# Element work of a gated MLP, taken two chunks at a time in stages, with engines kept in source order and the up projections ahead of the down projections

## The chip, the cores and the metric

The kernel runs on one core of a Trainium2 chip. Its time is the device time of one execution in microseconds. The engines are TensorE (PE, with its weight loads as PEld), VectorE (DVE), ScalarE (ACT), GpSimd (POOL) and SyncE (SP), whose queue issues nearly all DMAs. Each engine works through its own queue in the order in which the program was built.

## The reference: what is computed

An encoder of two layers on 256 tokens of width 1024. Each layer has a token mixer (pooling, windowed attention, gates, an output projection) and a gated MLP, each behind an RMSNorm and with a residual sum; a last RMSNorm follows. The change lies in the MLP, D_FF being 2816:

```python
def _conv_ffn(xn, w_up, conv_w, conv_b, w_down):
    a, gval = jnp.split(xn @ w_up, 2, axis=-1)
    a = lax.conv_general_dilated(a, conv_w[:, None, :], ...) + conv_b   # depthwise, width 3, over tokens
    return (jax.nn.gelu(a) * gval) @ w_down
```

All inputs and weights are float32, and the output is float32.

## The kernel before

**Split operands.** Every matmul operand is written as a high part and a low part (float32r each), and three products stand for one float32 product: high by high, high by low, low by high. A weight comes from HBM in loads of 1 MB (tile `raw`, three buffers, issued on SP), each cut into two pieces. A piece is split by one ACT cast (`wh`, L180) and one DVE subtraction (`wl`, L181), both 128x1024. `Weights.get(look)` returns the next piece and splits pieces up to `look` ahead, three as a rule and four in the up projections; five pieces can be alive at once, and `free` releases one. Some pieces have slots of their own in tiles that stand empty at that time.

**The MLP.** The up projections come in blocks of 512 columns: a0 to a4 and g0 to g4 (the convolved branch and the gate), and r5 with the last 256 columns of both. `by_rows` runs a block: four pieces, and for each piece 12 matmuls of 512 columns (two token halves, six products each). After each piece it calls `unit()`. `turn_up` then has DVE transpose the block's two PSUM tiles in 32x32 squares (`up_rows`, L1133), and when a gate block is done, `cross` moves the squares between partitions with 16 DMAs on SP, four with each unit (`up_turned`, L616). From then on channels are on partitions.

**Element work.** The 2816 channels are 22 chunks of 128. `up(f)` does one chunk: ACT copies the branch (L1152) and scales it with the middle tap (L1154), DVE adds the two outer taps (L1155, L1158); ACT squares (L1165), DVE (L1166), ACT takes tanh (L1169), DVE (L1170); DVE multiplies with the gate (L1174); ACT writes the high part (L1177) and DVE the low part (L1178) of the chunk, into a ring of 12 chunks. `CHUNKS` says after which unit each chunk is written into the program, whole, as one run of eleven instructions.

**Down projections.** `residual_mm` takes a chunk and a piece of `w_down` at a time, 12 matmuls of 512 columns again (L524 to L526), into four accumulators. The last four chunks are held, and finish the accumulators in segments (512 and 512 columns for the first half of the tokens, 512, 256 and 256 for the second); behind each segment the residual sum (DVE, L429), its squares (ACT, L431), and, at the end of a half, the norm (POOL L443, DVE L456) and TensorE's transposes of it (L465) follow. In layer 0, `begin_values` puts the first value products of layer 1 between the transposes; their four pieces have slots of their own.

**What sets the order.** The source is traced, and a scheduler then places the instructions on each engine by its own estimate of when each could run, so that the built order of ACT, DVE and PE is not that of the source. `ORDER` sets the order of blocks in the source: four down units (d0) stand between g2 and a3.

Of the kernel before, what the change touches and what calls it, by code (L numbers as in the profile page):

```python
# [10 lines left out]
F32 = mybir.dt.float32  # L11
F32R = mybir.dt.float32r
# [4 lines left out]
P = 128  # L17
# [64 lines left out]
class Weights:  # L82
# [114 lines left out]
    def get(self, look=LOOK):  # L197
# [10 lines left out]
def encoder(ctx, tc, x, w_in, w_pool, pool_scale, w_a, w_b, w_o, norm1, norm2, w_up, conv_w,  # L208
# [29 lines left out]
    for l in range(DEPTH):  # L238
        for g in range(NG):
            c0 = C_V + g * 512  # L240
            slots = (("m2", 0, 2), ("m2", 1, 2), ("ybig",), ("at2",)) if g == 0 else ()
            for j in range(2):
# [25 lines left out]
        for half in HALVES:  # L268
            half_of(w_a[l], 0, half, 2)
            half_of(w_in[l], C_GA, half, 2)  # L270
            half_of(w_b[l], 0, half, 1)
        for c in range(4):
            W.use(rows(w_o[l], c * 256))
        slots = (("v1",), ("ybig",), ("at2",))
        for kind, n in ORDER.split():
            n = int(n)
            for j in range(2):
# [304 lines left out]
    def run(gen):  # L582
        for _ in gen:
            pass

    def v_tile():
        return acc.tile([P, 512], F32, tag="acc", name="v_ps")

# [19 lines left out]
                visit()  # L608
        return ps

    def cross(out, in_):

        for i in range(4):
            for j in range(4):
                a, b = slice(32 * i, 32 * i + 32), slice(32 * j, 32 * j + 32)
                nc.sync.dma_start(out=out[b, i], in_=in_[a, j])  # L616
            yield
# [174 lines left out]
    for l in range(DEPTH):  # L792
# [318 lines left out]

        acth, actl = (
            [
                big.tile([P, n, 2, P], F32R, tag=f"{tag}{j}", name=f"act{tag}{j}")
                for j, n in enumerate((HPG, NH - HPG))
            ]
            for tag in "qk"
        )
        acts = {}

# [3 lines left out]
        def turn_up(kind, n, ps):  # L1124

            if kind != "g":
                pair[:] = (
                    big.tile([P, 4, 2, 2, 4, 32], F32, tag=tags[n % 2], name=name)
                    for tags, name in ((("at2", "ybig"), "up_rows"), (("xn", "v1"), "up_turned"))
                )  # L1130
            rows, out = (a[:, :, int(kind == "g")] for a in pair)
            for t in range(2):
                nc.vector.transpose(  # L1133
                    out=rows[:, :, t].rearrange("p j c r -> p c j r"),
                    in_=ps[t].rearrange("p (c j r) -> p c j r", c=4, j=4),
                )
            turned[kind, n] = out.rearrange("p i t c r -> p c t i r")
            if kind == "g":
                crossing.append(cross(pair[1], pair[0]))
            if kind == "r":  # L1140
                crossing.append(cross(out, rows))

        def blocks_in_order(a):

            return a.rearrange("p (i r t) -> p t i r", i=4, t=2)

        def up(f):
            w0, w1, w2, b = (prm[:, l, j * NF + f : j * NF + f + 1] for j in range(4))
            n, c = divmod(f, 4)
            av, gv = (turned["r", n][:, j + c] if n == 5 else turned[k, n][:, c] for k, j in (("a", 0), ("g", 2)))  # L1150
            a = sm.tile([P, S], F32, tag="u", name="a")
            nc.scalar.copy(out=blocks_in_order(a), in_=av)  # L1152
            y = sm.tile([P, S], F32, tag="s", name="y")
            nc.scalar.activation(y, a, AF.Identity, bias=b, scale=w1)  # L1154
            nc.vector.scalar_tensor_tensor(  # L1155
                out=y[:, 1:], in0=a[:, : S - 1], scalar=w0, in1=y[:, 1:], op0=ALU.mult, op1=ALU.add
            )
            nc.vector.scalar_tensor_tensor(  # L1158
                out=y[:, : S - 1], in0=a[:, 1:], scalar=w2, in1=y[:, : S - 1],
                op0=ALU.mult, op1=ALU.add,  # L1160
            )

            c = float(np.sqrt(2.0 / np.pi))
            y2 = sm.tile([P, S], F32, tag="us", name="y2")
            nc.scalar.activation(y2, y, AF.Square, scale=float(np.sqrt(0.044715)))  # L1165
            nc.vector.scalar_tensor_tensor(  # L1166
                out=y2, in0=y2, scalar=1.0, in1=y, op0=ALU.add, op1=ALU.mult
            )
            nc.scalar.activation(y2, y2, AF.Tanh, scale=c)  # L1169
            nc.vector.scalar_tensor_tensor(  # L1170
                out=y2, in0=y2, scalar=1.0, in1=y, op0=ALU.add, op1=ALU.mult
            )
            g = sm.tile([P, 2, P], F32, tag="p", bufs=3, name="g")
            nc.vector.tensor_mul(out=g.rearrange("p t (i r) -> p t i r", i=4), in0=blocks_in_order(y2), in1=gv)  # L1174
            n = f % NH
            ah, al = (x[n >= HPG][:, n - HPG * (n >= HPG)] for x in (acth, actl))
# [4 lines left out]
            acts[f] = (ah, al)  # L1181

        late = {}
        begun = []

        def begin_values():

            ps, held = v_tile(), [W.get() for _ in range(4)]
# [9 lines left out]
        count, chunk = 0, 0  # L1198

        def unit():  # L1200
            nonlocal count, chunk
            count += 1
            if crossing and next(crossing[0], "end") == "end":
                crossing.pop(0)
            while chunk < NF and CHUNKS[chunk] < count:
                up(chunk)
                chunk += 1

        for kind, n in ORDER.split():
            if kind == "d":  # L1210
                for _ in range(4):
                    next(down)
                    unit()
                continue
            if (kind, n) == ("a", "0"):
# [8 lines left out]
                ps = by_rows(x2, 4, unit, W.LOOK + 1)  # L1224
            n = int(n)
            turn_up(kind, n, ps)
        assert chunk == NF and not crossing
# [36 lines left out]
```

## Time and profile before

| | |
|---|---|
| median of 3 runs | 870.39 us (869.97 to 870.42) |
| profiled execution | 869.86 us, its span 868.1 us |
| granted TensorE clock | 0.999 |
| PE, PEld | 857.6 us, 723.4 us busy |
| DVE, ACT, POOL | 653.1, 484.6, 22.0 us busy |
| HBM read | 160.12 MB, 186 GB/s over the span |

The span reaches from the first to the last instruction of the profiled execution; what is around it is in the execution's time alone. Matmuls are pipelined, so a PE that is busy all the time may still lose time between matmuls: this is read from their starts. Rows of a timeline give the start in us from the span's start, the length in us, engine, source line, operation, tiles written and read, shapes and the count of merged instructions, then in brackets the idle time before and what ended it. Rows of groups give busy time, mean ns of one, then idle time before them and what ended it. An "SPq" row is the issue of a DMA.

### The profile page before, as it was taken

How to read it: one execution, taken by the hardware profiler on the slowest of the kernel's cores; microseconds unless marked ns; L12 is line 12 of the kernel's file. 1: busy time of each engine (PE TensorE's matmuls, PEld its weight loads, DVE VectorE, ACT ScalarE, POOL GpSimd, SP SyncE). 2: the span in 40 equal slices, each digit the busy share in tenths (PEclk: the TensorE clock that was granted, in tenths of full speed). 3: DMA queues.
4: the chain of work that ended last, by engine and by line, in shares of the span. 5: the costliest groups of instructions: out<-in, count | busy, mean ns of one | idle time of the engine just before them, and what ended most of it. 6: DMA issues, size and time to landing. Idle time of an engine off the chain costs nothing.

```text
span 868.1 us, 11702 instructions
## 1 busy us (share of the span) xinstructions
PE 857.6 (99%) x4234; PEld 723.4 (83%) x4234; DVE 653.1 (75%) x1016; ACT 484.6 (56%) x777; POOL 22.0 (3%) x53
## 2 busy tenths in 40 slices
PE   9999999999999999999999999999999999999997
PEld 7888988888888888888788889888888888888876
DVE  6998796756756797969965968775567758968796
ACT  7755554543634666566745555545445436756584
POOL 2020000000000000000000000000000000000000
PEclk9999999999999999999999999999999999999999
DMA  9676646665747777576746556556567377757761
GB/s 334 214 220 220 212 126 215 190 221 169 267 147 224 234 228 236 176 235 209 267 156 207 182 194 194 148 192 211 203 216 260 106 241 239 217 174 237 247 220 48
DMA packets 106942, 178.74 MB, mean 206 GB/s; under 512 B 7982, under 2 KB 49150, under 8 KB 106884
## 3 DMA queue, kind: packets, MB, share of 16 engines
q1 hardware_dynamic: 106372, 176.66, 61.9%
q0 software_dynamic: 496, 1.33, 0.6%
q8 instruction: 33, 0.54, 0.2%
q14 instruction: 25, 0.20, 0.1%
q10 hardware_dynamic: 16, 0.00, 0.0%
HBM read 160.12 MB, written 1.07 MB: 186 GB/s over the span
## 4 chain that ended last, share of the span: by engine, by line
PE 87%; DVE 7%; DMA 2%; SPq 1%; issue 1%; ACT 1%; POOL 0%; POOLq 0%; DVEq 0%; ACTq 0%
PE rows_ps L594 41%; PE proj_ps L497 14%; PE proj_ps L499 7%; PE v_ps L594 6%; DVE wl L181 4%; PE res_ps L525 3%; PE res_ps L526 3%; PE res_ps L524 3%; PE v_ps L784 3%; PE v_ps L697 1%; SPq L616 1%; DMA up_turned<-up_rows 1%; PE o_ps L975 1%; PE s_ps L918 1%; DVE y L1170 1%
## 5 line engine op out<-in xcount | busy, mean ns | idle before, releaser
L181 DVE TENSOR_TENSOR wl<-raw,wh 128x1024 fp32r<-128x1024 f32 x274 | 331.5, 1220 | 128.2 <-ACT wh L180 123.7
L180 ACT CAST wh<-raw 128x1024 fp32r<-128x1024 f32 x274 | 284.2, 1048 | 186.9 <-PE rows_ps L594 94.7
L594 PE MATMUL rows_ps<-wh,x 128*128 128x512 f32 x896 | 279.8, 391 | 0.0
L594 PEld LDWEIGHTS rows_ps<-wh,x 128*128 128x128 f32 x896 | 168.2, 188 | 34.3
L594 PE MATMUL rows_ps<-wl,x 128*128 128x512 f32 x448 | 174.8, 390 | 0.2
L497 PE MATMUL proj_ps<-x,wh 128*128 128x512 f32 x512 | 128.7, 393 | 0.0
L497 PEld LDWEIGHTS proj_ps<-x,wh 128*128 128x128 f32 x512 | 92.1, 189 | 16.4
L594 PEld LDWEIGHTS rows_ps<-wl,x 128*128 128x128 f32 x448 | 84.2, 188 | 18.4 <-DVE wl L181 1.1
L499 PEld LDWEIGHTS proj_ps<-x,wl 128*128 128x128 f32 x512 | 69.9, 190 | 5.1
L499 PE MATMUL proj_ps<-x,wl 128*128 128x256 f32 x512 | 71.6, 283 | 0.0
L525 PE MATMUL res_ps<-wl,actq 128*128 128x512 f32 (+1 forms) x184 | 70.4, 385 | 0.1
L526 PE MATMUL res_ps<-wh,actk 128*128 128x512 f32 (+1 forms) x184 | 70.2, 381 | 0.0
L524 PE MATMUL res_ps<-wh,actq 128*128 128x512 f32 (+1 forms) x184 | 64.8, 382 | 1.0 <-ACT wh L180 1.0
L1133 DVE STREAM_TRANSPOSE up_rows<-rows_ps 128x512 f32<-128x512 f32 x40 | 27.6, 705 | 25.3 <-PE rows_ps L594 21.6
L525 PEld LDWEIGHTS res_ps<-wl,actq 128*128 128x128 f32 x184 | 34.6, 188 | 8.8 <-DVE wl L181 2.2
L524 PEld LDWEIGHTS res_ps<-wh,actq 128*128 128x128 f32 x184 | 34.5, 188 | 8.4 <-ACT wh L180 1.8
L594 PE MATMUL rows_ps<-wh,po 128*128 128x512 f32 x128 | 40.1, 389 | 0.0
L526 PEld LDWEIGHTS res_ps<-wh,actk 128*128 128x128 f32 x184 | 34.6, 188 | 6.3
L1154 ACT ACTIVATE y<-a,prm 128x256 f32<-128x256 f32 x44 | 25.1, 593 | 14.1 <-DVE y L1170 14.1
L1165 ACT ACTIVATE y<-y 128x256 f32<-128x256 f32 x44 | 18.3, 416 | 26.0 <-DVE y L1158 25.8
L594 PEld LDWEIGHTS rows_ps<-wh,po 128*128 128x128 f32 x128 | 24.0, 188 | 5.0
L1177 ACT ACTIVATE actq<-g 128x256 fp32r<-128x256 f32 x44 | 17.6, 415 | 18.7 <-DVE g L1174 18.5
(203 smaller groups left out, 1107.2 us busy)
## 6 DMA issues: line engine op xcount, KB each, us to landing
raw<-in_w_in_dram SPq DMA_DIRECT2D x58, 1024.0 KB, 6.2
raw<-in_w_up_dram SPq DMA_DIRECT2D x40, 1024.0 KB, 5.9
raw<-in_w_down_dram SPq DMA_DIRECT2D x22, 1024.0 KB, 6.7
up_turned<-up_rows SPq DMA_DIRECT2D x160, 64.0 KB, 3.9
raw<-in_w_a_dram SPq DMA_DIRECT2D x8, 1024.0 KB, 4.9
raw<-in_w_o_dram SPq DMA_DIRECT2D x8, 1024.0 KB
pt<-rows SPq DMA_DIRECT2D x64, 64.0 KB, 4.8
raw<-in_w_b_dram SPq DMA_DIRECT2D x4, 1024.0 KB
```

Source lines behind the costliest of these rows:

```text
L180: lambda: nc.scalar.copy(out=h, in_=src),
L181: lambda: nc.vector.tensor_sub(out=l, in0=src, in1=h.bitcast(F32)),
L497: nc.tensor.matmul(ps, wh(k), x2[:, k], start=(k == 0), stop=False)
L499: nc.tensor.matmul(ps[:, 1], wl(k), x2[:, k, 0], start=False, stop=(k == nk - 1))
L524: nc.tensor.matmul(ps, ah, wh, start=first, stop=False)
L525: nc.tensor.matmul(ps, ah, wl, start=False, stop=False)
L526: nc.tensor.matmul(ps, al, wh, start=False, stop=last)
L594: nc.tensor.matmul(ps, x2[:, 2 * n + j, part, t, :], w[:, j, :], start=(n + m == 0), stop=(n == of - 1 and m == 5),)
L784: nc.tensor.matmul(ps[t], a[:, k, t, :], w[:, j, :], start=(k + m == 0), stop=(k == KD - 1 and m == 2),)
L1133: nc.vector.transpose(out=rows[:, :, t].rearrange("p j c r -> p c j r"), in_=ps[t].rearrange("p (c j r) -> p c j r", c=4, j=4),)
L1154: nc.scalar.activation(y, a, AF.Identity, bias=b, scale=w1)
L1165: nc.scalar.activation(y2, y, AF.Square, scale=float(np.sqrt(0.044715)))
```

## The change

- `ORDER` puts all up blocks ahead of the down units, and a new entry v0 behind g0.
- `v0` (layer 0 only) takes two of the four pieces of layer 1's first value columns there, into the tile `m2`, where `begin_values` finds them; the other two stay at the end.
- The element work becomes `two_up(f)`: two chunks in four stages, one stage with each unit. Copies, taps and the multiplication with the gate stay one instruction per chunk; the square, tanh, the two operations behind them, and both halves of the split become one instruction for both chunks, 512 wide. `TWOS` lists the units at which a pair begins.
- The ring holds 16 chunks, the last four in the tiles `v0` and `gates`.
- `keep_order` ties each instruction on PE, ACT and DVE to the one before it in the source, from the first block to the last unit of d4, for order alone, without a semaphore. SP and POOL are left to the scheduler, and so is what follows d4.
- In block a0, `ahead` splits one more piece with each unit. The crossing of r5 begins one unit later.

```diff
-ORDER = "a0 g0 a1 g1 a2 g2 d0 a3 g3 a4 g4 r5 d1 d2 d3 d4"
-CHUNKS = (*range(13, 36, 2), 41, 43, 45, 47, 50, 51, 53, 54, 56, 57)
+ORDER = "a0 g0 v0 a1 g1 a2 g2 a3 g3 a4 g4 r5 d0 d1 d2 d3 d4"
+RING = 16
+TWOS = (16, 20, 24, 28, 32, 36, 39, 43, 47, 51, 55)
...
+    def ahead(self, n):
+        self._split(self.n_got + n)
...
+    def keep_order(engines=("PE", "Activation", "DVE")):
+
+        traced = nc.cur_bb.bb.instructions
+        first = traced[-1]
+        yield
+        start = next(k for k in reversed(range(len(traced))) if traced[k] is first) + 1
+        before = {}
+        for i in traced[start:]:
+            e = i.engine.name
+            if e in engines:
+                if e in before:
+                    info = mybir.DependencyInfo(mybir.DependencyClass.NoSync, mybir.DependencyReason.DATA)
+                    tc.add_manual_dep(i, before[e].name, info, reason="source order")
+                before[e] = i
...
+        def two_up(f):
+
+            a = sm.tile([P, 2, S], F32, tag="u", name="a")
+            yg = sm.tile([P, 4, S], F32, tag="s", name="yg")
+            for j in range(2):
+                w0, w1, w2, b = (prm[:, l, i * NF + f + j : i * NF + f + j + 1] for i in range(4))
+                av, _ = rows_of(f + j)
+                aj, y = a[:, j], yg[:, j]
+                nc.scalar.copy(out=blocks_in_order(aj), in_=av)
+                nc.scalar.activation(y, aj, AF.Identity, bias=b, scale=w1)
+                nc.vector.scalar_tensor_tensor(
+                    out=y[:, 1:], in0=aj[:, : S - 1], scalar=w0, in1=y[:, 1:], op0=ALU.mult, op1=ALU.add
+                )
+                nc.vector.scalar_tensor_tensor(
+                    out=y[:, : S - 1], in0=aj[:, 1:], scalar=w2, in1=y[:, : S - 1],
+                    op0=ALU.mult, op1=ALU.add,
+                )
+            yield
 
             c = float(np.sqrt(2.0 / np.pi))
+            y, g = yg[:, 0:2], yg[:, 2:4]
+            y2 = sm.tile([P, 2, S], F32, tag="us", name="y2")
             nc.scalar.activation(y2, y, AF.Square, scale=float(np.sqrt(0.044715)))
             nc.vector.scalar_tensor_tensor(
                 out=y2, in0=y2, scalar=1.0, in1=y, op0=ALU.add, op1=ALU.mult
             )
+            yield
+
             nc.scalar.activation(y2, y2, AF.Tanh, scale=c)
             nc.vector.scalar_tensor_tensor(
                 out=y2, in0=y2, scalar=1.0, in1=y, op0=ALU.add, op1=ALU.mult
             )
+            for j in range(2):
+                _, gv = rows_of(f + j)
+                gj = g[:, j].rearrange("p (t i r) -> p t i r", t=2, i=4)
+                nc.vector.tensor_mul(out=gj, in0=blocks_in_order(y2[:, j]), in1=gv)
+            yield
...
+            nc.scalar.mul(out=ah, in_=g, mul=0.5)
             nc.vector.scalar_tensor_tensor(
                 out=al, in0=g, scalar=0.5, in1=ah.bitcast(F32), op0=ALU.mult, op1=ALU.subtract
             )
...
+            yield
...
         def unit():
-            nonlocal count, chunk
+            nonlocal count
             count += 1
             if crossing and next(crossing[0], "end") == "end":
                 crossing.pop(0)
-            while chunk < NF and CHUNKS[chunk] < count:
-                up(chunk)
-                chunk += 1
+            if count in TWOS:
+                open_two.append(two_up(2 * len(twos)))
+                twos.append(count)
+            for two in open_two:
+                next(two, None)
...
+            if kind == "v":
+                if l + 1 < DEPTH:
+                    late["pieces"] = [W.get() for _ in range(2)]
+                continue
...
                 for k in range(4):
+                    W.ahead(k + 1)
                     v_sum(ps[1], x2, 1, k, held[k])
                     unit()
```

More of the change, by code (lines that the diff above doesn't have):

```diff
@@ L241, in encoder @@
             slots = (("m2", 0, 2), ("m2", 1, 2), ("ybig",), ("at2",)) if g == 0 else ()
-            for j in range(2):
+            for j in range(l > 0 and g == 0, 2):
                 tag = "k1" if l == 0 and g == 1 and j == 0 else None
@@ L276, in encoder @@
             n = int(n)
+            if kind == "v":
+                if l + 1 < DEPTH:
+                    W.use(rows(w_in[l + 1], 0, 4, C_V, 512), (("m2", 0, 2), ("m2", 1, 2)))
+                continue
             for j in range(2):
@@ L609, in by_rows, with cross @@
         return ps
-    def cross(out, in_):
+    def cross(out, in_, after=0):
+        for _ in range(after):
+            yield
         for i in range(4):
@@ L1113, in encoder @@
             [
-                big.tile([P, n, 2, P], F32R, tag=f"{tag}{j}", name=f"act{tag}{j}")
-                for j, n in enumerate((HPG, NH - HPG))
+                big.tile([P, n, 2, P], F32R, tag=tag, name=f"act{tag}")
+                for tag, n in zip(tags, (HPG, NH - HPG, HPG))
             ]
-            for tag in "qk"
+            for tags in (("q0", "q1", "v0"), ("k0", "k1", "gates"))
         )
@@ L1140, in turn_up, with rows_of @@
             if kind == "r":
-                crossing.append(cross(out, rows))
+                crossing.append(cross(out, rows, 1))
         def blocks_in_order(a):
             return a.rearrange("p (i r t) -> p t i r", i=4, t=2)
-        def up(f):
-            w0, w1, w2, b = (prm[:, l, j * NF + f : j * NF + f + 1] for j in range(4))
+        def rows_of(f):
             n, c = divmod(f, 4)
[L1150 to L1161, printed above, removed]
+            return (turned["r", n][:, j + c] if n == 5 else turned[k, n][:, c] for k, j in (("a", 0), ("g", 2)))
@@ L1163, in up @@
             c = float(np.sqrt(2.0 / np.pi))
-            y2 = sm.tile([P, S], F32, tag="us", name="y2")
+            y, g = yg[:, 0:2], yg[:, 2:4]
+            y2 = sm.tile([P, 2, S], F32, tag="us", name="y2")
             nc.scalar.activation(y2, y, AF.Square, scale=float(np.sqrt(0.044715)))
@@ L1172, in up @@
             )
[L1173 to L1176, printed above, removed]
+            for j in range(2):
[3 more added lines that the diff above has]
+            yield
+            n = f % RING
+            m = (n >= HPG) + (n >= NH)
+            n -= (0, HPG, NH)[m]
+            ah, al = (x[m][:, n : n + 2] for x in (acth, actl))
+            g = g.rearrange("p c (t m) -> p c t m", t=2)
             nc.scalar.mul(out=ah, in_=g, mul=0.5)
@@ L1180, in up @@
             )
-            acts[f] = (ah, al)
+            for j in range(2):
+                acts[f + j] = (ah[:, j], al[:, j])
+            yield
         late = {}
@@ L1186, in begin_values @@
         def begin_values():
-            ps, held = v_tile(), [W.get() for _ in range(4)]
+            ps, held = v_tile(), late["pieces"] + [W.get() for _ in range(2)]
             for n in range(3):
@@ L1197, in encoder @@
         )
-        count, chunk = 0, 0
+        count, twos, open_two = 0, [], []
         def unit():
-            nonlocal count, chunk
+            nonlocal count
             count += 1
@@ L1204, in unit @@
                 crossing.pop(0)
-            while chunk < NF and CHUNKS[chunk] < count:
-                up(chunk)
-                chunk += 1
+            if count in TWOS:
[3 more added lines that the diff above has]
+                next(two, None)
+        ordered = keep_order()
+        next(ordered)
         for kind, n in ORDER.split():
@@ L1214, in encoder @@
                 continue
+            if kind == "v":
+                if l + 1 < DEPTH:
+                    late["pieces"] = [W.get() for _ in range(2)]
+                continue
             if (kind, n) == ("a", "0"):
@@ L1226, in encoder @@
             turn_up(kind, n, ps)
-        assert chunk == NF and not crossing
+        next(ordered, None)
+        assert 2 * len(twos) == NF and not crossing
         if l + 1 < DEPTH:
```

## The prediction

> **What bounds the kernel now.** I read the page first: the engines' shares, then the chain of waits.
>
> ```profile
> span 868.1 us, 11702 instructions
> PE 857.6 (99%) x4234; PEld 723.4 (83%) x4234; DVE 653.1 (75%) x1016; ACT 484.6 (56%) x777; POOL 22.0 (3%) x53
> PE 87%; DVE 7%; DMA 2%; SPq 1%; issue 1%; ACT 1%; POOL 0%; POOLq 0%; DVEq 0%; ACTq 0%
> ```
>
> TensorE carries 87% of the chain. The change leaves every matmul of the kernel in place, so it can win only what TensorE loses between matmuls. The 13% that the chain gives to others are not that loss: while TensorE has weights in stock, a chain through VectorE costs it nothing. So I looked at stages, and then at starts of matmuls.
>
> ```profile
> 263.10:320.00 56.90, 56.90 (x253) 47.15 (x252) 42.14 (x61) 30.34 (x46) 0.00 (x0) 1.00 0.76 241
> 382.00:437.00 55.00, 52.70 (x243) 42.71 (x242) 51.65 (x92) 38.22 (x69) 2.49 (x4) 1.00 0.70 234
> ...
> 263.12 54.40 PE rows_ps L594 x240
> ```
>
> The stage rows give length, then busy time of PE, PEld, DVE, ACT, POOL, the clock, DMA. Early in layer 0's MLP TensorE never stops; late in it VectorE is busy 51.65 of 55.00 us and TensorE falls short. The third line, a piece of the chain, gives the pitch of undisturbed 512-column matmuls: 54.40/240 = 0.2267 us. A weight piece serves 12 of them, 2.72 us; I call that a unit. An MLP has 66 units (44 up, 22 down). Now the loss:
>
> ```profile
> 262.96 0.39 PE L594 MATMUL rows_ps<-wh,x 128*128 128x512 f32 x1
> 432.18 0.28 PE L526 MATMUL res_ps<-wh,actk 128*128 128x256 f32 x1
> 434.20 0.41 PE L465 MATMUL xt_ps<-ident,xn 128*128 128x128 f32 x2 [1.75 <-DVE xn L456]
> 691.00 0.39 PE L594 MATMUL rows_ps<-wh,x 128*128 128x512 f32 x1
> 858.92 0.28 PE L524 MATMUL res_ps<-wh,actq 128*128 128x256 f32 x1
> ```
>
> Unit 5 of layer 0 begins at 262.96. Up to the last 256-column matmul before the norm's transposes stand, by the code, 58 units of 12 and three held segments of 12, 732 matmuls of 512 columns (165.9 us), and eleven of 256. In layer 1 the first 256-column matmul starts at 858.92: 167.92 us, 2.0 over 165.9. In layer 0, 169.22 less 165.9 less eleven at 0.12 (half the columns) leaves 2.0 too. After that TensorE waits for the norm, 434.20 − 432.18 − 0.12 = 1.9 us. So 2.0 + 1.9 + 2.0 = 5.9 us are there to be had, 0.7%, unless something new is broken.
>
> Who causes the 2.0?
>
> ```profile
> 415.91 0.39 PE L526 MATMUL res_ps<-wh,actk 128*128 128x512 f32 x1
> 416.78 1.19 PE L524 MATMUL res_ps<-wh,actq 128*128 128x512 f32 x4 [0.48 <-ACT wh L180]
> 418.38 0.40 PE L526 MATMUL res_ps<-wh,actk 128*128 128x512 f32 x1
> ...
> 344.53 1.03 ACT L180 CAST wh<-raw 128x1024 fp32r<-128x1024 f32 x1
> 348.84 0.72 DVE L1133 STREAM_TRANSPOSE up_rows<-rows_ps 128x512 f32<-128x512 f32 x1 [3.76 <-PE rows_ps L594]
> 349.48 1.18 DVE L181 TENSOR_TENSOR wl<-raw,wh 128x1024 fp32r<-128x1024 f32 x1
> ```
>
> From 415.91 to 418.38 six matmuls take 2.47 us where 1.36 would do: 1.1 us lost for a late split (wh on ACT, wl on DVE). The other kind is in the last rows: ACT's half of a split ends at 345.56, but a transpose put at the head of DVE's queue waits 3.76 us for TensorE, and DVE's half comes at 349.48. Both are matters of order and backlog on ACT and DVE, which the change rewrites.
>
> **The change, part by part.**
>
> *Splits, transposes, element work in source order.* In by_rows a piece is split four units ahead, and its buffer (five of them) is that of the piece just finished. So in source order a transpose waiting for the end of unit u stands ahead of a split that needs the buffer of unit u anyway: nothing that could run is behind it. The 3.76 us wait before a ready split cannot recur in this form. What is left is whether DVE keeps up.
>
> ```profile
> L181 DVE TENSOR_TENSOR wl<-raw,wh 128x1024 fp32r<-128x1024 f32 x274 | 331.5, 1220 | 128.2 <-ACT wh L180 123.7
> L180 ACT CAST wh<-raw 128x1024 fp32r<-128x1024 f32 x274 | 284.2, 1048 | 186.9 <-PE rows_ps L594 94.7
> L1133 DVE STREAM_TRANSPOSE up_rows<-rows_ps 128x512 f32<-128x512 f32 x40 | 27.6, 705 | 25.3 <-PE rows_ps L594 21.6
> L1158 DVE SCALAR_TENSOR_TENSOR y<-a,prm,y 128x255 f32<-128x255 f32 x44 | 20.9, 480 | 0.7
> L1166 DVE SCALAR_TENSOR_TENSOR y<-y,y 128x256 f32<-128x256 f32 x44 | 18.2, 418 | 1.8 <-ACT y L1165 1.7
> L869 DVE SCALAR_TENSOR_TENSOR pd<-us,u 128x512 f32<-128x512 f32 x8 | 5.5, 686 | 0.0
> 383.62 0.75 DVE L1170 SCALAR_TENSOR_TENSOR y<-y,y 128x256 f32<-128x256 f32 x2
> 422.55 3.49 DVE L181 TENSOR_TENSOR wl<-raw,wh 128x1024 fp32r<-128x1024 f32 x3
> ```
>
> Four units (10.88 us) now hold four splits, two transposes and one pair of chunks: four convolution steps, three merged 512-wide operations (priced by L869, the same operation at that width), two multiplies. By whole durations: 4×1.22 + 2×0.705 + 4×0.48 + 3×0.686 + 2×0.418 = 11.1, so DVE would fall behind by 0.2 per four units, about 1.3 us over the six pairs begun at units 16 to 36. But the last two rows show that queued instructions overlap: three splits in 3.49 us are 1.14 each, two 256-wide operations in 0.75 are 0.33 each, 0.085 less than alone. Taking that off all fifteen leaves 9.8, a full us to spare. Stage one beside a block's end can put DVE some 1.5 us late, made good in the next units; a split is due 4×2.72 − 1.05 − 1.22 = 8.6 us after it may begin. Either price hides. In the down phase transposes fall away after unit 44, and pairs come four units apart; DVE has 2 us more. I therefore price the MLP stalls at nothing but a 0.1 us bubble or two.
>
> The Trainium skill (Perfetto Trace Analysis, Optimizing Scalar/DVE Operations) puts DVE's overhead per instruction on SBUF at about 60 ns, the profiled one at about twice that since half overlaps the next; by it each merge saves 60 ns, by the durations above 2×418 − 686 = 150. The overlap in the trace agrees with the page's kind of price. The sum is the same by both, since DVE is hidden by both.
>
> *Value pieces of layer 1 split early (v0).* Two splits (2.4 us DVE, 2.1 ACT) and a 1 MB load move from the end of layer 0's MLP to units 4 to 9, where there is no element work:
>
> ```profile
> 269.69 1.23 DVE L181 TENSOR_TENSOR wl<-raw,wh 128x1024 fp32r<-128x1024 f32 x1 [1.50 <-ACT wh L180]
> 425.62 2.00 ACT L180 CAST m<-raw 128x1024 fp32r<-128x1024 f32 x2 [2.10 <-DMA raw<-in_w_in_dram]
> 428.95 1.05 ACT L180 CAST ybig<-raw 128x1024 fp32r<-128x1024 f32 x1 [1.33 <-DMA raw<-in_w_in_dram]
> 430.86 0.62 ACT L431 ACTIVATE junk<-h 128x512 f32<-128x512 f32 x1
> 428.99 1.28 DVE L429 TENSOR_TENSOR h<-res_ps,h 128x512 f32<-128x512 f32 x2
> 433.57 0.49 DVE L456 SCALAR_TENSOR_TENSOR xn<-h,rstd,gain 128x256 f32<-128x256 f32 x1 [0.44 <-POOL rstd L443]
> ```
>
> DVE has 1.50 us idle per unit there, so two units absorb them; without that cover they would cost 2.4. On SP the load goes ahead of block a1's weights, wanted only at unit 9 (273.9). At the end, the squares (junk) that follow the residual sums of 428.99 are held until 430.86 by casts whose load came late (428.95). The two remaining pieces now take the place of m's, ready by 425.62, and those casts end by 427.6, so the squares start with the sums, about 1.2 us sooner; the rest comes from the split backlog that is gone. The mixer's end runs the same residual code without such casts:
>
> ```profile
> 248.62 0.28 PE L526 MATMUL res_ps<-wh,m 128*128 128x256 f32 x1
> 248.74 0.60 PE L465 MATMUL xt_ps<-ident,xn 128*128 128x128 f32 x4
> ```
>
> There the transposes follow at 0.12, no wait at all. Bounds of this term: 1.2 to 1.9; I take 1.6, nearer the mixer's row.
>
> *Free edits.* The larger ring only lets down projections follow all ups. The down matmuls moved are as many as before. Order on SP and POOL is not imposed.
>
> Sum: 2.0 + 2.0 + 1.6 = 5.6 us. The profiled run took 869.86 (span 868.1 and 1.8 around it); 864.3 by that run. The median is 870.39, 0.5 above it: 864.8.
>
> **Rivals.**
>
> *The norm wait stays* (scheduling behind the loop is not pinned, and ybig's casts may still stand ahead of the squares): gain 4.0 less bubbles, 866.6. For: the same queue mixes both. Against: the load is one place earlier.
>
> *Slower: ACT held by a crossing.* The copy that opens a pair waits for the crossing DMAs of its block, and in forced order the casts queue behind it.
>
> ```profile
> 273.55 1.31 DVE L1133 STREAM_TRANSPOSE up_rows<-rows_ps 128x512 f32<-128x512 f32 x2
> 280.51 6.19 SPq L616 DMA_DIRECT2D up_turned<-up_rows  x8
> 372.36 0.72 DVE L1133 STREAM_TRANSPOSE up_rows<-rows_ps 128x512 f32<-128x512 f32 x1 [0.64 <-PE rows_ps L594]
> 386.63 5.81 SPq L616 DMA_DIRECT2D up_turned<-up_rows  x8
> up_turned<-up_rows SPq DMA_DIRECT2D x160, 64.0 KB, 3.9
> L1154 ACT ACTIVATE y<-a,prm 128x256 f32<-128x256 f32 x44 | 25.1, 593 | 14.1 <-DVE y L1170 14.1
> L1152 ACT COPY a<-up_turned 128x256 f32<-128x256 f32 x44 | 17.0, 416 | 1.6 <-DMA up_turned<-up_rows 1.6
> ```
>
> With 3.9 us to landing, block 0 crossed 280.51 + 6.19 + 3.9 − 274.86 = 15.7 us after its transposes, block 4 took 386.63 + 5.81 + 3.9 − 373.08 = 23.3, SP being held by loads that waited for splits. Blocks 3 and 4 have the least time: transposed behind units 32 and 40, opened at 39 and 47. Unit 47 begins at 262.96 + 42×2.72 = 377.2, its copy may run from 378.3, behind a cast; unit 40 ends at 360.9, the transposes with a lag of 1.5 near 363.7. With 15.7 the copy waits 1.1; with 23.3 until 387.0. Then stage one (2.0: two of 0.593, two of 0.416) and a split (2.3) bring piece 51 at 391.3, wanted at 388.1: 3.2 us lost, and by the same count 0.5 at unit 39. Two layers: 7.4 lost against 5.6 won, 872.2. It turns slower from a crossing of about 22.4 us. Against it: with DVE less behind, the loads that held SP come free sooner. By the Trainium skill's rule that ACT and DVE are strict first-in-first-out queues (Perfetto Trace Analysis, Tensor Engine Instruction), nothing could pass the waiting copy; the 3.76 us row agrees for DVE.
>
> *Nothing happens*: order is not what is missing, the pairs lag as chunks did, 870.
>
> **How the numbers follow.** Forecast 0.70 (864.2 to 866.0), norm wait stays 0.13, nothing 0.05, crossing 0.12. The range runs from 863.5 (all 5.9, and a us of small bubbles around the norms) to 868.0 (norm wait kept and a third of the stalls), which leaves out the last two cases and some tail. About 0.2% (1.7 us) can be told from no change: faster 0.83, same 0.05, slower 0.12.
>
> **What would show it.** Right: between unit 5 and the first 256-column matmul about 166 us in both layers; the transpose wait after layer 0's last held segment under 0.5; DVE's split waiting for ACT, never PE for DVE. Norm rival: 1.75 stays on that row. Crossing rival: ACT's copy waits for up_turned by more than 5 us and PE waits for wh about units 43 and 51. Wrong altogether: PE waits of a kind not listed, or a changed pitch.

## The result, and the profile after

The changed kernel takes 863.91 us in the median (863.62 to 864.34), the kernel before, run beside it, 870.28 us. The ratio is 0.9928, with a 95% interval of 0.991 to 0.9945: faster by 6.4 us. Its profiled execution took 863.69 us, with a span of 861.6. All ratios below are to the kernel before, measured beside each kernel.

First the page of the kernel after: instructions, the engines' busy shares, and the chain of waits by engine.

```profile
span 861.6 us, 11559 instructions
PE 854.1 (99%) x4234; PEld 724.0 (84%) x4234; DVE 651.3 (76%) x950; ACT 487.5 (57%) x711; POOL 20.2 (2%) x53
PE 98%; DMA 0%; ACT 0%; SPq 0%; issue 0%; DVE 0%; POOLq 0%; POOL 0%; DVEq 0%; ACTq 0%
```

TensorE carries 98% of the chain instead of 87%, with the same 4234 matmuls. ACT and DVE have 66 instructions less each, but their busy times have hardly moved (DVE 653.1 to 651.3 us).

The stages of layer 0's MLP in the kernel after (length, then busy time of PE, PEld, DVE, ACT and POOL, the granted clock, DMA share and GB/s):

```profile
263.10:320.00 56.90, 56.90 (x253) 47.12 (x252) 44.20 (x57) 32.56 (x41) 0.00 (x0) 1.00 0.81 267
320.00:382.00 62.00, 62.00 (x276) 51.32 (x275) 59.51 (x90) 45.81 (x66) 0.00 (x0) 1.00 0.73 241
382.00:431.00 49.00, 49.00 (x227) 40.93 (x226) 35.51 (x51) 27.37 (x38) 0.99 (x3) 1.00 0.61 212
```

TensorE is busy throughout. VectorE's crowded stretch is no longer the last one (51.65 of 55.00 us before) but the middle one, 59.51 of 62.00 (46.95 before), and there it costs nothing. Now the starts that the prediction measured by, in the timeline of TensorE after:

```profile
262.95 0.39 PE L617 MATMUL rows_ps<-wh,x 128*128 128x512 f32 x1
428.87 0.28 PE L532 MATMUL res_ps<-wh,actq 128*128 128x256 f32 x1
430.18 0.28 PE L534 MATMUL res_ps<-wh,actk 128*128 128x256 f32 x1
430.30 0.60 PE L473 MATMUL xt_ps<-ident,xn 128*128 128x128 f32 x4
686.47 0.39 PE L617 MATMUL rows_ps<-wh,x 128*128 128x512 f32 x1
852.39 0.28 PE L532 MATMUL res_ps<-wh,actq 128*128 128x256 f32 x1
```

From unit 5 to the first 256-column matmul: 428.87 − 262.95 = 165.92 us and 852.39 − 686.47 = 165.92 us, the time of 732 undisturbed matmuls in both layers. Both losses of 2.0 are gone to the last hundredth. The norm's transposes follow the last segment by 0.12 (430.18 to 430.30), so the wait of 1.9 is gone too. That is 5.9 of the span's 6.5 us; the last 0.6 are small bubbles of 0.1 to 0.2 us, which stood between the transposes and in the value products that follow them.

### The profile page after: what moved, and what is told of

It is laid out like the page before. It is cut to its first block, busy times and chain, and to the rows that moved or that the text cites. A ratio compares the mean times of both kernels' runs of the same rounds, so it can differ in the third digit from the quotient of the medians.

```text
span 861.6 us, 11559 instructions
## 1 busy us (share of the span) xinstructions
PE 854.1 (99%) x4234; PEld 724.0 (84%) x4234; DVE 651.3 (76%) x950; ACT 487.5 (57%) x711; POOL 20.2 (2%) x53
## 4 chain that ended last, share of the span: by engine, by line
PE 98%; DMA 0%; ACT 0%; SPq 0%; issue 0%; DVE 0%; POOLq 0%; POOL 0%; DVEq 0%; ACTq 0%
PE rows_ps L617 43%; PE proj_ps L505 13%; PE proj_ps L507 7%; PE v_ps L617 6%; PE res_ps L532 6%; PE res_ps L534 6%; PE res_ps L533 6%; PE v_ps L809 3%; PE v_ps L722 1%; PE o_ps L1000 1%; PE s_ps L943 1%; PE o_ps L996 1%; PE s_ps L938 1%; PE xt_ps L473 1%; PE pool_ps L499 0%; PE pool_ps L498 0%
## 5 line engine op out<-in xcount | busy, mean ns | idle before, releaser
L617 PEld LDWEIGHTS rows_ps<-wl,x 128*128 128x128 f32 x448 | 84.1, 188 | 17.3
L532 PE MATMUL res_ps<-wh,actq 128*128 128x512 f32 (+1 forms) x152 | 57.5, 378 | 0.0
L533 PE MATMUL res_ps<-wl,actq 128*128 128x512 f32 (+1 forms) x152 | 57.4, 378 | 0.0
L534 PE MATMUL res_ps<-wh,actk 128*128 128x512 f32 (+1 forms) x152 | 57.4, 378 | 0.0
L533 PEld LDWEIGHTS res_ps<-wl,actq 128*128 128x128 f32 x152 | 28.6, 188 | 5.4
L532 PEld LDWEIGHTS res_ps<-wh,actq 128*128 128x128 f32 x152 | 28.6, 188 | 5.4
L534 PEld LDWEIGHTS res_ps<-wh,actk 128*128 128x128 f32 x152 | 28.6, 188 | 5.3
L439 ACT ACTIVATE junk<-h 128x512 f32<-128x512 f32 (+1 forms) x20 | 10.9, 547 | 30.8 <-DVE h L437 30.8
L1185 ACT ACTIVATE yg<-a,prm 128x256 f32<-128x256 f32 x44 | 26.6, 604 | 1.5
L532 PE MATMUL res_ps<-wh,m 128*128 128x512 f32 (+1 forms) x72 | 26.9, 374 | 0.0
```

Of the source, the lines that this page charges most:

```text
L439: nc.scalar.activation(junk[:, 0 : cc.stop - cc.start], h[:, t, cc], AF.Square, scale=D**-0.5, accum_out=ss[:, n : n + 1],)
L532: nc.tensor.matmul(ps, ah, wh, start=first, stop=False)
L533: nc.tensor.matmul(ps, ah, wl, start=False, stop=False)
L534: nc.tensor.matmul(ps, al, wh, start=False, stop=last)
L617: nc.tensor.matmul(ps, x2[:, 2 * n + j, part, t, :], w[:, j, :], start=(n + m == 0), stop=(n == of - 1 and m == 5),)
L1185: nc.scalar.activation(y, aj, AF.Identity, bias=b, scale=w1)
```

## The experiments

Three kinds: parts of the change taken out, parts of it put alone on the kernel before, and the slower rival brought about.

### The forced order taken out of the kernel after

```diff
-        ordered = keep_order()
-        next(ordered)
+        ordered = iter(())
```

> The changed kernel without the ties between instructions: pairs, stages, early value pieces and block order as they are, the order on each engine again the scheduler's. Theory O (order): the stalls inside the MLPs (2.0 us a layer before) come from transposes and element work that stand ahead of splits that could run; without the ties 1 to 2 us a layer return, 866 to 868 us, with PE waiting for wh or wl, and DVE waiting at transposes for several us at a time. Theory L (load): what mattered is that VectorE has less to do and the down units come last; the time stays within 0.5 us of 863.9.

Measured: 871.47 us (869.35 to 874.21), ratio 1.001 (0.9996 to 1.0024). The whole gain is gone. TensorE loses 3.0 us per layer, in one stall; the norm wait stays away. The profiled execution, at 869.35 us, has these stalls at the full clock; what makes others up to 5 us longer is in the last section. The stall's rows in layer 0, from the timelines of ACT, DVE and PE without the order:

```profile
366.72 1.03 ACT L181 CAST wh<-raw 128x1024 fp32r<-128x1024 f32 x1
370.55 0.72 DVE L1158 STREAM_TRANSPOSE up_rows<-rows_ps 128x512 f32<-128x512 f32 x1 [5.52 <-DMA up_turned<-up_rows]
374.24 1.22 DVE L182 TENSOR_TENSOR wl<-raw,wh 128x1024 fp32r<-128x1024 f32 x1
375.51 0.50 PE L533 MATMUL res_ps<-wl,actq 128*128 128x512 f32 x1 [2.74 <-DVE wl L182]
```

ACT's half of the split ends at 367.75, DVE's half starts at 374.24. Between them the scheduler put a transpose that waits 5.52 us for a DMA, and then stage-one work. This is the same kind of stall as the 3.76 us in the kernel before. The stages alone don't cure it.

### The forced order alone, on the kernel before

```diff
+        ordered = keep_order()
+        next(ordered)
...
+        next(ordered, None)
```

> The kernel before with nothing but the ties: element work a whole chunk at a time, CHUNKS, d0 and the value pieces where they were. Theory O: the 2.0 us a layer inside the MLPs go, the norm's wait of 1.9 us stays: 866.4 us (865.8 to 867.2). Theory L: whole chunks in source order make ACT and DVE wait for each other eleven times a chunk, VectorE stays behind, 870 us or slower.

Measured: 948.24 us, ratio 1.0895 (1.0876 to 1.0914): 78 us slower. Theory O was wrong by its whole sign; what came is theory L, far beyond its 870. Three rows of the timeline of DVE, then a wait of ACT for DVE and one of DVE for ACT (total us, times, longest):

```profile
301.22 0.43 DVE L1181 SCALAR_TENSOR_TENSOR y<-y,y 128x256 f32<-128x256 f32 x1 [0.55 <-ACT y L1180]
303.85 1.31 DVE L1148 STREAM_TRANSPOSE up_rows<-rows_ps 128x512 f32<-128x512 f32 x2
318.51 1.31 DVE L1148 STREAM_TRANSPOSE up_rows<-rows_ps 128x512 f32<-128x512 f32 x2
...
ACT y L1180 <- DVE y L1173: 70.6, 44, 2.1
DVE y L1181 <- ACT y L1180: 24.1, 44, 0.8
```

In source order a chunk is a chain of eleven instructions that goes back and forth between ACT and DVE, and nothing else may pass while one waits for the other. A block's four pieces and the two chunks beside them need 318.51 − 303.85 = 14.66 us on DVE, 3.54 of them idle in seven waits for ACT; TensorE needs 4 × 2.72 = 10.88. The loss recurs with every block, and behind the stalls the granted clock falls too (0.977 in the mean of the profiled execution). The scheduler's order of before was not only a nuisance: it filled these gaps.

### All four stages in one unit, order kept

```diff
-                next(two, None)
+                run(two)
```

> The changed kernel, source order kept, but all four stages of a pair in one unit. Each pair then puts some 4.8 us of VectorE work, with ACT and VectorE waiting for each other at four changes of hand (about 0.6 us each), between two splits. A split may be 8.6 us late in the up phase and 5.9 in the down phase, so theory O with its slack expects no more than 1 us over both layers, 863.9 to 864.9 us. A rival: the stages are what keeps VectorE from idling, and without them it falls behind from pair to pair, 867 us or more.

Measured: 897.51 us, ratio 1.0312 (1.0296 to 1.0327). Theory O was wrong again, for the same reason; the rival (867 us or more) came. DVE's timeline with one stage per pair:

```profile
339.93 1.30 DVE L1158 STREAM_TRANSPOSE up_rows<-rows_ps 128x512 f32<-128x512 f32 x2
...
348.34 0.69 DVE L1199 SCALAR_TENSOR_TENSOR y<-y,yg 128x512 f32<-128x512 f32 x1 [0.76 <-ACT y L1198]
349.73 0.69 DVE L1205 SCALAR_TENSOR_TENSOR y<-y,yg 128x512 f32<-128x512 f32 x1 [0.70 <-ACT y L1204]
...
351.92 0.69 DVE L1220 SCALAR_TENSOR_TENSOR actk<-yg,actq 128x512 fp32r<-128x512 f32 x1 [0.70 <-ACT actq L1219]
352.53 1.31 DVE L1158 STREAM_TRANSPOSE up_rows<-rows_ps 128x512 f32<-128x512 f32 x2
```

Three hand-overs from ACT leave DVE idle for 2.16 us per pair. The period is 352.53 − 339.93 = 12.60 us against 10.88. The same place in the kernel after:

```profile
305.04 1.23 DVE L182 TENSOR_TENSOR wl<-raw,wh 128x1024 fp32r<-128x1024 f32 x1 [0.62 <-ACT wh L181]
...
315.92 1.23 DVE L182 TENSOR_TENSOR wl<-raw,wh 128x1024 fp32r<-128x1024 f32 x1 [0.62 <-ACT wh L181]
```

The period is 10.88 us, and DVE's only idle time in it is 0.62: with one stage in each unit, ACT's part runs while DVE does splits. So stages are not a matter of lateness that is made good later; they set whether DVE's work fits into the period at all.

### Stages and order for single chunks, on the kernel before

The kernel before with the order forced and each chunk's eleven instructions in four stages, one per unit. No pairs, no merged instructions, ring of 12, d0 in its old place, value pieces late, and no early splits in block a0.

```diff
+            yield            # behind the taps, the square and the tanh steps of up(f)
...
-                up(chunk)
+                open_up.append(up(chunk))
+            for one_up in open_up:
+                next(one_up, None)
```

> The kernel before with the ties, and with the element work of each single chunk in four stages, one with each unit: no pairs, no merging, ring of 12, d0 and value pieces where they were. Stages with order are then what the gain is made of: nothing lost inside the MLPs, 863.9 to 864.6 us (the single chunk's sequence keeps ACT and VectorE busy at once, as in the pairs that were not merged). Rival: two chunks in a stage are needed to fill the waits between ACT and VectorE; then VectorE falls behind as with whole chunks, 875 us or more.

Measured: 868.93 us (868.71 to 869.57), ratio 0.9986 (0.9977 to 0.9996), between both expectations. By the starts, the MLP loses 2.0 us in each layer, and all of it in one place, which the kernel before doesn't have. DVE's and PE's timelines:

```profile
263.17 0.72 DVE L1148 STREAM_TRANSPOSE up_rows<-v_ps 128x512 f32<-128x512 f32 x1 [0.64 <-PE v_ps L609]
263.81 3.45 DVE L181 TENSOR_TENSOR wl<-raw,wh 128x1024 fp32r<-128x1024 f32 x3
265.05 0.50 PE L609 MATMUL rows_ps<-wl,x 128*128 128x512 f32 x1 [1.69 <-DVE wl L181]
```

The two transposes of block a0 wait for TensorE at the head of DVE's queue, and three splits that could have run long before stand behind them. It is the early splits of block a0 that are missing.

### The early splits of block a0 taken out of the kernel after

```diff
-                    W.ahead(k + 1)
```

> The kernel after without the early splits of block a0 (the splitting of one more piece with each of its four units), everything else as it is. Theory A, source order needs them: with single chunks in stages and the order kept, TensorE waited 1.85 us at 262.97 for the first low half of block g0, because two transposes of a0 that wait for TensorE stood ahead of it on DVE, and the same in layer 1 (2.0 per layer in all). Without the early splits the pairs should show the same wait: 1.8 to 2.0 us per layer at unit 5, 863.9 + 3.7 to 4.0 = 867.5 to 867.9, ratio about 0.997. Rival B, the stall belongs to the single chunks or to the down units left between: no wait at unit 5, 863.4 to 864.4. The prediction priced this edit at nothing and did not say what hides it.

Measured: 867.95 us (867.64 to 868.33), ratio 0.9969 (0.9958 to 0.998). By the starts it loses 2.03 and 1.99 us, at unit 5 of each layer, and nothing elsewhere. ACT's, DVE's and PE's timelines:

```profile
258.82 3.89 ACT L181 CAST wh<-raw 128x1024 fp32r<-128x1024 f32 x4
263.81 0.72 DVE L1158 STREAM_TRANSPOSE up_rows<-v_ps 128x512 f32<-128x512 f32 x1 [0.64 <-PE v_ps L617]
264.45 4.59 DVE L182 TENSOR_TENSOR wl<-raw,wh 128x1024 fp32r<-128x1024 f32 x4
265.69 0.50 PE L617 MATMUL rows_ps<-wl,x 128*128 128x512 f32 x1 [1.69 <-DVE wl L182]
```

ACT's halves of the four splits are done one by one from 259.9 to 262.7. In the kernel after, DVE takes its halves at once, and the transposes of a0 follow at 264.90:

```profile
259.22 4.63 DVE L182 TENSOR_TENSOR wl<-raw,wh 128x1024 fp32r<-128x1024 f32 x4 [0.26 <-ACT wh L181]
```

Theory A holds. One line, about which the prediction says nothing, is worth 4.0 us of the 6.4. It also closes the case of the single chunks: in the MLP they lose 2.03 and 1.98, the same as the pairs without these splits. What is left between the two, about 1 us, lies at the norm at the end of layer 0 and in the value products behind it.

### Value pieces late again, with the order and without it

```diff
-ORDER = "a0 g0 v0 a1 g1 a2 g2 a3 g3 a4 g4 r5 d0 d1 d2 d3 d4"
+ORDER = "a0 g0 a1 g1 a2 g2 a3 g3 a4 g4 r5 d0 d1 d2 d3 d4"
...
-            ps, held = v_tile(), late["pieces"] + [W.get() for _ in range(2)]
+            ps, held = v_tile(), [W.get() for _ in range(4)]
```

> The changed kernel with all four value pieces of layer 1 at the end of layer 0's MLP again. If the early pieces removed the norm's wait (my term of 1.6 us): TensorE waits 1.2 to 1.9 us for xn at the end of layer 0, 865.1 to 865.8 us. If the wait went because the split backlog went: under 0.5 us of wait, 863.9 to 864.4 us.

> The changed kernel without the ties and with all four value pieces at the end of layer 0's MLP. Without the ties but with early pieces the norm's wait was gone and 3.0 us a layer were lost inside the MLPs; with the ties and late pieces nothing was lost anywhere. If either one suffices against the norm's wait, it comes back only here: 1.2 to 1.9 us at the end of layer 0, about 873 us. If pairs or up-first already remove it, no wait there and about 871 us.

Measured: with the order 863.86 us, ratio 0.9926 (0.9911 to 0.994); without it 871.32 us, ratio 1.0015 (1.0002 to 1.0027). The norm wait is 0 in both. DVE's timeline with late pieces and the order:

```profile
420.38 2.35 DVE L182 TENSOR_TENSOR m<-raw,m 128x1024 fp32r<-128x1024 f32 x2
...
424.92 0.69 DVE L437 TENSOR_TENSOR h<-res_ps,h 128x512 f32<-128x512 f32 x1
426.31 0.69 DVE L437 TENSOR_TENSOR h<-res_ps,h 128x512 f32<-128x512 f32 x1 [0.71 <-PE res_ps L534]
```

And two rows of the kernel before, the issue of the value pieces' loads and the last element work of its layer 0 on DVE:

```profile
420.16 12.78 SPq L120 DMA_DIRECT2D raw<-in_w_in_dram  x5
422.21 0.42 DVE L1178 SCALAR_TENSOR_TENSOR actk<-g,actq 128x256 fp32r<-128x256 f32 x1
```

All four pieces are still split at the end, but those of m start at 420.38 instead of 426.71, and the residual sums no longer stand behind them (428.99 before). By these rows, what had kept them late before was the element work of the last chunks, which ran on DVE until 422.6 with the splits between and behind it. A load needs a buffer that a split has freed: that of m was issued only at 420.16, when the split begun at 418.91 had ended (with late pieces and the order, at 409.61), and ACT's cast of m then waited 2.10 us for it. So the wait went with that backlog (argued from the rows, no run takes it alone), and not with the two pieces that moved. Neither the order nor the moved pieces is needed for it; of the staging, the pairs and the ring no run isolates which one is. With single chunks in stages 0.74 us of it stay, and there it is order, behind the part that is tied: a residual sum waits 3.35 us for TensorE at the head of DVE's queue, and the splits of `ybig` and `at`, cast by 425.1, run only behind it, at 429.38 and 430.51, ahead of the norm.

### Merged instructions as two again; d0 back between g2 and a3

```diff
-            nc.scalar.activation(y2, y2, AF.Tanh, scale=c)
+            for j in range(2):
+                nc.scalar.activation(y2[:, j], y2[:, j], AF.Tanh, scale=c)
...
-ORDER = "a0 g0 v0 a1 g1 a2 g2 a3 g3 a4 g4 r5 d0 d1 d2 d3 d4"
-TWOS = (16, 20, 24, 28, 32, 36, 39, 43, 47, 51, 55)
+ORDER = "a0 g0 v0 a1 g1 a2 g2 d0 a3 g3 a4 g4 r5 d1 d2 d3 d4"
+TWOS = (16, 20, 24, 28, 32, 36, 43, 47, 51, 54, 57)
```

(The first hunk stands for all six merged instructions; the second and third are the other kernel.)

> The changed kernel, same stages and order, but each merged 512-wide instruction again as two 256-wide ones. VectorE idles 0.62 us in four units of the changed kernel. By start-to-start prices three merges save 3 x (2 x 0.33 - 0.60) = 0.2 us of VectorE in four units, by whole durations 3 x 0.15 = 0.45: both less than 0.62, so theory O expects no change (863.9 +- 0.4) with VectorE's idle time down to 0.2 to 0.4 us in four units. Theory L expects stalls: 865 us or more.

> The changed kernel with d0 between g2 and a3 again, and the units at which the later pairs begin moved along (43, 47, 51, 54, 57). Theory O: which projections come first does not matter as long as VectorE keeps up, 863.9 +- 0.4 us. Theory L: the up-first order is what frees VectorE in the down phase, 865 us or more, with waits for wl near the end of the down units.

Measured: 863.84 us, ratio 0.9924 (0.991 to 0.9939), and 864.15 us, ratio 0.9926 (0.9911 to 0.9941). Neither loses anything between unit 5 and the first 256-column matmul. So neither part, taken out alone, has an effect on the time. VectorE's idle time in four units fell from 0.62 only to 0.54, not to 0.2 to 0.4. DVE's timeline of the kernel after, then of the one that is not merged:

```profile
310.34 0.68 DVE L1199 SCALAR_TENSOR_TENSOR y<-y,yg 128x512 f32<-128x512 f32 x1
310.94 1.22 DVE L182 TENSOR_TENSOR wl<-raw,wh 128x1024 fp32r<-128x1024 f32 x1
```

```profile
310.33 0.75 DVE L1201 SCALAR_TENSOR_TENSOR y<-y,yg 128x256 f32<-128x256 f32 x2
311.00 1.22 DVE L182 TENSOR_TENSOR wl<-raw,wh 128x1024 fp32r<-128x1024 f32 x1
```

The next split starts 0.60 us after a merged operation and 0.67 after the two: a merge saves DVE 0.07 us.

### The slower rival brought about: crossings begun one, two and three units later

```diff
-                crossing.append(cross(pair[1], pair[0]))
+                crossing.append(cross(pair[1], pair[0], 3))
```

(2 and 1 in the other two kernels.)

> The changed kernel with the crossing of every gate block started three units (8.2 us) later. Crossings end 14.8 us after their transposes in the changed kernel; here 23. This prices the slower rival of the prediction: it gave 3.2 us lost near unit 47 and 0.5 near unit 39 in each layer for 23.3, that is 7.4 us, 871.3. Worked again from the changed kernel's trace, where the copy of pair 8 stood at 376.98 and piece 51 is wanted at 388.1: 1.3 us there, 0.2 near unit 39, 3 us in both layers, 867 us (865.4 to 868). If a held copy cost nothing (casts not behind it): 863.9.

> The changed kernel with the crossing of each gate block started two units (5.4 us) later. Where VectorE makes good only 0.6 to 1.1 us in four units, the holds of ACT add up from pair to pair: some 1, 4, 4, 4.5 and 5.5 us, 18 in all less about 5 made good, against 8.6 of slack: 3 to 5 us lost a layer, 870 to 875 us. If each hold is made good before the next, as the prediction had it: 864 us.

> The same with the crossing one unit (2.7 us) later: holds of about 0, 1, 1, 2 and 3 us, under 8.6 even if nothing is made good: 863.9 to 864.5 us. Above 866 the slack is smaller than the count says.

Measured: three later 883.97 us, ratio 1.0147 (1.013 to 1.0164); two later 863.21 us, ratio 0.9923 (0.9908 to 0.9938); one later 863.39 us, ratio 0.9923 (0.9908 to 0.9938). ACT's copies that open a pair, in the timelines of three later and then of two later:

```profile
297.64 0.42 ACT L1184 COPY a<-up_turned 128x256 f32<-128x256 f32 x1 [3.57 <-DMA up_turned<-up_rows]
322.29 0.42 ACT L1184 COPY a<-up_turned 128x256 f32<-128x256 f32 x1 [4.36 <-DMA up_turned<-up_rows]
347.31 0.42 ACT L1184 COPY a<-up_turned 128x256 f32<-128x256 f32 x1 [4.74 <-DMA raw<-in_w_up_dram]
371.22 0.42 ACT L1184 COPY a<-up_turned 128x256 f32<-128x256 f32 x1 [4.58 <-DMA up_turned<-up_rows]
```

```profile
294.70 0.42 ACT L1184 COPY a<-up_turned 128x256 f32<-128x256 f32 x1
316.46 0.42 ACT L1184 COPY a<-up_turned 128x256 f32<-128x256 f32 x1
338.22 0.42 ACT L1184 COPY a<-up_turned 128x256 f32<-128x256 f32 x1
...
383.22 0.42 ACT L1184 COPY a<-up_turned 128x256 f32<-128x256 f32 x1 [4.12 <-DMA up_turned<-up_rows]
```

(The third row names a weight load, but the last four DMAs of the crossing reached their semaphores between 346.58 and 347.20, so the crossing held that copy too.) The first three copies are eight units apart, 21.76 us; the fourth begins seven units later, 19.04. Two later, the first three start at that pitch; two holds come at the end (1.50 and 4.12 us) and cost TensorE nothing. Three later, they are 24.65, 25.02 and 23.91 us apart. ACT's casts and DVE's work queue behind a held copy, so the next transposes come late, and the next crossing later still: the transposes of g1, g2 and g3 start 3.5, 6.4 and 9.6 us later than in the kernel after (300.61, 325.25 and 350.26 against 297.13, 318.89 and 340.65). The lag is not made good but grows, until TensorE, whose first wait comes there, has used up its stock of pieces at 349.7. Three later is 17 us above what I expected; two later is near the 864 of the other case, some 7 below the sum of the holds. My account of holds that add up held for three units and fell for two: by these rows the lag grew where the early crossings landed after their pairs were due, and not where only the last ones did. Three later also costs more than the holds, as its next rows show (TensorE's timeline, then a stretch with the granted clock behind POOL's column):

```profile
374.20 0.49 PE L617 MATMUL rows_ps<-wh,x 128*128 128x512 f32 x1 [2.36 <-ACT wh L181]
375.46 0.79 PE L617 MATMUL rows_ps<-wl,x 128*128 128x512 f32 x1 [0.77 <-DVE wl L182]
...
371.40:381.50 10.10, 6.98 (x17) 4.99 (x17) 9.09 (x15) 7.54 (x12) 0.00 (x0) 0.66 0.37 126
```

Behind two waits of 2.36 and 0.77 us the clock fell to a mean of 0.66, and the matmuls came 0.427 us apart until 381.2.

## Why the prediction was right, and where it was not

- **What is to be had: 2.0 + 1.9 + 2.0.** Right. All three went to nothing, and 0.6 us of bubbles with them; in the stages above TensorE waits for nobody. The profiled run was put at 864.3 and took 863.69; the median was put at 864.8, its main case at 864.2 to 866.0, and came out at 863.91, 0.3 below that case. What the sum lacked is 0.3 of the norm wait and the 0.6 of bubbles.
- **The stalls are a matter of order and backlog.** Right, and the order is needed: without it 3.0 us per layer come back in the form of that 3.76 us row.
- **"Nothing that could run is behind it."** The step that failed without showing in the sum: here the prediction was right by luck, since a line that it never weighed covers the place. It holds in `by_rows`. At block a0 it doesn't: a0 works on pieces with slots of their own, so splits for g0 could run, and source order puts a0's transposes ahead of them. Only the early splits move them forward; without them the price is 4.0 us, and the median would have been the 867.95 of that run. The prediction lists "free edits" and leaves this one out.
- **DVE's load, 9.8 to 11.1 us of 10.88.** The rows give 10.88 less 0.62 idle, 10.26 us, between both prices. But lateness "made good in the next units" was the wrong picture of why that is enough: when ACT and DVE must wait for each other within a unit, 2.16 us per pair are added in every period (12.60 us), and nothing is made good.
- **Norm wait, 1.6 us, by moving two value pieces.** The size was low (1.9 was taken), and the cause was wrong: late pieces give 863.86. By the rows, the part that the prediction called "the split backlog that is gone" was all of it; that the term came near is luck.
- **Merging, and the block order that the larger ring allows, are worth nothing.** Right: 863.84 without the merged instructions, 864.15 with d0 back. Of the two prices of a merge, 150 ns by the rows and 60 by the Trainium skill (Perfetto Trace Analysis, "Optimizing Scalar/DVE Operations"), the second is nearer: the starts above give 70 ns.
- **Rival of the crossing.** Its condition did not come about. In the kernel after, the longest hold on these copies was 0.16 us. The mechanism is real, the sum was not. The transposes of g4 with two later, and of g3 with three later:

```profile
364.64 1.31 DVE L1158 STREAM_TRANSPOSE up_rows<-rows_ps 128x512 f32<-128x512 f32 x2
```

```profile
350.26 1.31 DVE L1158 STREAM_TRANSPOSE up_rows<-rows_ps 128x512 f32<-128x512 f32 x2
```

  From the end of a block's transposes to its landing, 383.22 − 365.95 = 17.3 us (g4, two later) cost nothing, while 371.22 − 351.57 = 19.7 us (g3, three later) already belong to a kernel that is 20 us slower than the one after. The prediction turned slower only from 22.4 (22.9, if both of its holds shrink as it counts them), and took two holds per layer at 3.7 us together, where the holds recur in every block, lag adds to lag, and the clock drops.

## What to carry to other kernels

In this kernel, forcing source order on the engines was worth something only once the source was pipelined: no instruction may stand right behind the one on another engine that it waits for, and every instruction that could run early must stand ahead of the waits. Here order alone cost 78 us, order with unstaged pairs 27, order with stages but without one line of early splits lost 4.0 of the 6.4, and the three together, on pairs, won it all (single chunks with all three were not run). So price an order by walking each queue for "what stands behind this wait that could run now", at the ends of a loop as well as in its middle, and price waits inside a period as a rate.

## What the runs showed of the hardware

Whether a wait of 2.9 us halved TensorE's clock changed from one execution to the next. The two kernels without the order have the same stall of 2.9 us at the same place. The stretch behind it, first in the one with early value pieces and then in the one with late ones (length, busy PE, PEld, DVE, ACT, POOL, granted clock, DMA share, GB/s):

```profile
375.50:381.80 6.30, 6.29 (x28) 5.21 (x29) 6.30 (x10) 5.42 (x7) 0.00 (x0) 1.00 0.57 175
```

```profile
375.50:381.80 6.30, 6.13 (x15) 4.82 (x16) 6.30 (x11) 5.25 (x7) 0.00 (x0) 0.51 0.46 172
```

In the same 6.3 us, 28 matmuls start in one profile and 15 in the other, at granted clocks of 1.00 and 0.51. Each kernel has this stall once in each layer, and their executions fall into groups: seven of twenty at 869.35 to 869.54 us, nine at 871.15 to 872.85, four at 873.95 to 874.21. The first profile (869.35) has the full clock behind both of its stalls, the second (873.95) has 0.51 and 0.73 over the 6.3 us behind its two; that the middle group has one such fall is inferred. That is why the two have wide ranges, while the kernel before, beside them, stays within 1.6 us. The Trainium skill (TensorE: Matmul & The Clock Gate, "What's actually happening") has the clock at half after an idle window of about 3.4 us that runs freely; the chance from one execution to the next agrees with that, and the runs add that 2.9 us of waiting, less than the window, can be enough. One profile shows both outcomes: with all four stages in one unit, the clock is 1.00 from 402 to 408 us, behind waits of 2.34 and 0.76, and 0.50 from 842 to 848, behind waits of 2.37 and 0.46. The half clock lasts longer or shorter: in the profile of 873.95 the MLPs lose 5.9 and 4.6 us where the other loses 3.0 in each. So a stall of this size cost its length, half as much again, or twice its length. The stalls of 1.85 us without early splits left the clock at 1.00 in both layers of their profile.
